# Early convolution blocks copied out of PSUM, keys rounded and half of the masked tiles made on VectorE, and four groups of matmuls set later

## The chip, the cores and the metric

The kernel runs on one core of a Trainium2 chip. The metric is the device time of one execution in microseconds (us), as the median of a few runs. The engines are named as in the profile: PE is TensorE's matmul, PEld its weight load, DVE is VectorE, ACT is ScalarE, POOL is GpSimd and SP is SyncE, which here issues most of the DMAs.

## The reference

One layer of a hybrid backbone on 1024 latent tokens and 256 context tokens of width 1024, in float32. The normed and modulated tokens go through one input projection, whose columns belong to two groups. Group A is a gated DeltaNet of 4 heads of 128 in two scan directions, group B is a two-dimensional neighbourhood attention of 8 heads of 64.

```python
h = modulate(rms_norm(x, w), shift, scale)        # 1280 x 1024
p = h @ w_in                                      # q, k, v, z, a, b of group A; q, k, v of group B
# group A
q, k, v = split(silu(conv5(p_qkv)))               # depthwise, 5 taps, centred, context and latent apart
k = k / sqrt(sum(k * k) + EPS)
g = -exp(A_log) * softplus(a + dt_bias);  beta = sigmoid(b)
decay = exp(gam_i - gam_j) where i >= j, else 0   # gam: running sum of g within a chunk
m = where(strict, (k * beta) @ k.T * decay, 0)
u, w = solve(eye + m, [v * beta, k * beta * exp(gam)])   # one triangular system a chunk
# then a scan over the chunks, forward and backward
# group B
q, k = rms_norm(q) * 64 ** -0.5, rms_norm(k)      # heads of 64, then the windowed softmax
```

Behind that come an output projection, a gated residual and a SwiGLU. The change concerns the stage up to about 400 us: the input projection, the preparation of the triangular systems, and what runs beside them.

## The kernel before

**The in-projection.** Tokens lie along the free axis, features on the partitions. The modulated input is held as two float32r parts, `hh` (rounded) and `hl` (the rest), and so is each weight tile, `whi` and `wlo`; a product is three matmuls, hi by hi, hi by lo and lo by hi (`mm_part`, L413). `Block` makes 128 output columns for all tokens, in PSUM tiles `blk` of 256, 512 and 512 tokens (q and nq: only the two of 512). `Wide` makes 256 columns with the tokens on the partitions. The jobs run in this order: k0 and k1 together, k2, k3, z's second half, then nk0 to nk2, nv's first half, nk3, q0 to q3, nq0 to nq3 and the rest. The letters q, k, v, z are of group A, nq, nk, nv of group B.

**A block's life.** `prefetch` loads the raw weight into `wraw` (one buffer only), ScalarE casts it to `whi` (L203), POOL subtracts to get `wlo` (L204); for a `Wide` job two loads into the same `wraw` are cast to `zw` (L601) and subtracted (L602). The next load into `wraw` waits for the cast and the subtraction of the one before. `evac` takes the sums out of PSUM into `cacc`; for q, k and v it also does the convolution, centre tap first, then four more taps. While `len(psum) == 1`, that is for k0 to k3, ScalarE scales out of PSUM into `cacc` (L446) and VectorE reads the four outer taps from PSUM, per segment (L455); for later blocks ScalarE copies into `cr` (L461) and VectorE does all five taps from there (L465, L469). `silu`, `norm` and `finish` follow one or two jobs later. For nk, `norm` sums squares on PE (L502), takes a logarithm (L503) and an exponential (L507) on ScalarE, scales on VectorE (L510), and splits into float16 parts: cast on ScalarE (L515), subtraction on VectorE (L516). For k, `finish` transposes (L537) and multiplies keys with keys (L561, copied by ScalarE at L562), and POOL with VectorE sum the diagonal.

**Banks.** Up to z's end one pool of 8 PSUM banks serves everything. From nk0 on, `blk` has 4 banks, `m` 2 and `pr` 2.

**The background work.** Generators step along between the groups of matmuls: each `bg.step` of the job loop runs a generator to its next `yield`, and a `yield` with nothing else lets one group of the job's matmuls pass (an empty step). `decay_tables` forms the decays and multiplies them on PE (L842). `block_inverses` makes masked tiles `rc` of the two parts GH and GL of the decays (`rhs`, L865, 12 of them, on POOL), a product of each pair (L878) and an exponential on ScalarE (L880) into WK and W, then masks on VectorE (L885 to L892), transposes into N (L900, copied at L902), an elimination of 30 pairs of VectorE instructions on N (L910, L912), and transposes out of N (L922, copied to WK at L926). `preps` prepares the chunks: `fx` and `y` tiles, decay products (L1003) and exponentials (L1008), a product kk by e on VectorE (L1011), products with fx (L1024) and a short series of `y` products (L1035). A second generator, `modulation`, forms the second half of the adaLN vector: VectorE accumulates eight `wad` tiles into `acc2` (L236, L238), and PE sums it over the partitions against ones (L223).

Every engine works through its instructions in the order in which a scheduler puts them; PE, VectorE and ScalarE wait on semaphores for one another, and nothing overtakes on an engine.

## Time and profile before

| what | us |
|---|---|
| runs, median (of 3) | 1512.97 |
| runs, lowest and highest | 1512.54, 1517.85 |
| the profiled execution: span | 1510.6 |
| PE busy in the span | 1462.2 (97%) |
| VectorE, ScalarE, POOL busy | 996.8, 703.5, 236.7 |

The profiled execution's own time outside the profiler isn't recorded, so its span stands for it; the median of the runs lies 2.4 us above the span. A row of the timeline has the start, the duration, the engine, line and operation, the output and inputs, and in brackets the idle time before it with what ended that. A row of the waits has what PE was about to run, whose end it waited for, and the total, the number and the longest wait.

### The profile page before, as it was taken

The numbers are of one execution on the slowest core, as the hardware profiler recorded it, in microseconds if no ns is written. First come the engines' busy times: TensorE is split into PE (matmuls) and PEld (weight loads), VectorE is DVE, ScalarE is ACT, GpSimd is POOL, SyncE is SP. The second block draws the span as 40 slices with busy tenths as digits, with TensorE's granted clock in tenths as the row PEclk, the third lists the DMA queues.
The fourth block names the chain that finished last, engine by engine and source line by source line (L and its number), as shares of the span: only waits on it lengthen the run. The fifth ranks groups of instructions, "written<-read, shape, count | busy, mean of one in ns | idle before, by whom it ended". The sixth has DMA issues, their size and how long they took to land.

```text
span 1510.6 us, 23890 instructions
## 1 busy us (share of the span) xinstructions
PE 1462.2 (97%) x8702; PEld 1223.5 (81%) x8702; DVE 996.8 (66%) x1716; ACT 703.5 (47%) x1389; POOL 236.7 (16%) x286
## 2 busy tenths in 40 slices
PE   6999999999999998999999999999999999999998
PEld 3788797877788877887878888888888888888887
DVE  5773589875463745778867389766665567598652
ACT  5453442456663246656853284333333334354440
POOL 1054601456652201111210000000000000000000
PEclk9999999999999999999999999999999999999999
DMA  9274122778665569998539205433333335798742
GB/s 389 75 215 143 54 78 72 244 222 248 195 191 174 157 187 291 290 263 279 163 112 343 79 28 166 141 105 105 105 105 105 105 105 174 260 360 279 251 140 84
DMA packets 205398, 267.36 MB, mean 177 GB/s; under 512 B 15968, under 2 KB 113760, under 8 KB 204256
## 3 DMA queue, kind: packets, MB, share of 16 engines
q1 hardware_dynamic: 197680, 260.01, 53.2%
q10 hardware_dynamic: 7600, 5.81, 1.2%
q8 instruction: 69, 1.13, 0.3%
q14 instruction: 49, 0.40, 0.1%
HBM read 201.02 MB, written 68.94 MB: 179 GB/s over the span
## 4 chain that ended last, share of the span: by engine, by line
PE 51%; ACT 1%; DVE 1%; issue 0%; DMA 0%; POOL 0%; DVEq 0%; POOLq 0%; ACTq 0%
PE ps L1398 28%; PE ps L1741 14%; PE ps L1527 3%; PE ps L1375 1%; PE ps L1549 1%; PE sc L332 1%; PE sc L322 1%; PE sc L309 1%; PE ps L1252 0%; PE ps L1261 0%; DMA z<-z_d 0%; ACT sq L1302 0%; ACT bt L315 0%; DVE bt L313 0%; PE ps L223 0%
## 5 line engine op out<-in xcount | busy, mean ns | idle before, releaser
L1459 ACT CAST uhi<-wq 128x512 fp32r<-128x512 f32 x101 | 61.3, 622 | 135.9 <-issue 84.6
L413 PE MATMUL blk<-hh,whi 128*128 128x512 f32 (+1 forms) x410 | 121.0, 389 | 1.6 <-ACT kk L562 1.4
L1459 ACT CAST uhi<-ws 128x512 fp32r<-128x512 f32 x91 | 54.0, 621 | 146.3 <-PE ps L1398 91.4
L413 PE MATMUL blk<-hl,whi 128*128 128x512 f32 (+1 forms) x410 | 113.4, 370 | 0.3 <-DVE hl L729 0.3
L609 PE MATMUL blk<-zw,hh 128*128 128x256 f32 (+1 forms) x576 | 112.3, 289 | 1.0 <-ACT cr L461 1.0
L413 PE MATMUL blk<-hh,wlo 128*128 128x512 f32 (+1 forms) x410 | 112.0, 370 | 0.6 <-POOL wlo L204 0.6
L1460 DVE TENSOR_TENSOR ulo<-wq,uhi 128x512 fp32r<-128x512 f32 x101 | 67.6, 688 | 59.1 <-ACT uhi L1459 32.7
L1398 PE MATMUL ps<-hT,uhi 128*128 128x512 f32 x336 | 103.7, 390 | 0.0
L1398 PE MATMUL ps<-lT,uhi 128*128 128x512 f32 x336 | 103.4, 389 | 0.0
L1398 PE MATMUL ps<-hT,ulo 128*128 128x512 f32 x336 | 103.4, 389 | 0.0
L609 PEld LDWEIGHTS blk<-zw,hh 128*128 128x128 f32 x576 | 90.7, 189 | 4.1 <-ACT cr L461 1.4
L1398 PE MATMUL ps<-hB,uhi 128*128 128x512 f32 x288 | 89.1, 390 | 0.0
L1398 PE MATMUL ps<-lB,uhi 128*128 128x512 f32 x288 | 88.7, 389 | 0.0
L1398 PE MATMUL ps<-hB,ulo 128*128 128x512 f32 x288 | 88.7, 389 | 0.0
L413 PEld LDWEIGHTS blk<-hh,wlo 128*128 128x128 f32 x410 | 71.0, 188 | 14.8 <-POOL wlo L204 0.9
L413 PEld LDWEIGHTS blk<-hl,whi 128*128 128x128 f32 x410 | 71.2, 188 | 14.4 <-DVE hl L729 0.8
L609 PE MATMUL blk<-zw,hl 128*128 128x256 f32 (+1 forms) x288 | 81.9, 284 | 0.0
L413 PEld LDWEIGHTS blk<-hh,whi 128*128 128x128 f32 x410 | 67.6, 190 | 16.8 <-issue 3.8
L204 POOL TENSOR_TENSOR wlo<-wraw,whi 128x1024 fp32r<-128x1024 f32 x18 | 44.8, 2488 | 186.8 <-ACT whi L203 186.5
L1398 PEld LDWEIGHTS ps<-lT,uhi 128*128 128x128 f32 x336 | 63.1, 188 | 13.1
L1398 PEld LDWEIGHTS ps<-hT,ulo 128*128 128x128 f32 x336 | 63.1, 188 | 13.1
L1398 PEld LDWEIGHTS ps<-hT,uhi 128*128 128x128 f32 x336 | 62.9, 188 | 13.0
(361 smaller groups left out, 3500.7 us busy)
## 6 DMA issues: line engine op xcount, KB each, us to landing
wq<-w_fo SPq DMA_DIRECT2D x99, 256.0 KB, 4.2
wq<-w_gu SPq DMA_DIRECT2D x88, 256.0 KB, 2.9
wad<-wa SPq DMA_DIRECT2D x64, 256.0 KB, 4.3
bt<-rpb SPq DMA_DIRECT2D x64, 192.0 KB, 3.9
t_d<-g SPq DMA_DIRECT2D x22, 512.0 KB, 3.5
fr<-t_d SPq DMA_DIRECT2D x44, 256.0 KB, 4.9
f_d<-g SPq DMA_DIRECT2D x33, 256.0 KB, 2.1
fr<-f_d SPq DMA_DIRECT2D x33, 256.0 KB, 4.2
```

Of the source, the lines that this page charges most:

```text
L204: lo_engine.tensor_tensor(o, r, h.bitcast(F32), OP.subtract)
L309: s = pe.matmul(sc[:, u * 640 + n0:u * 640 + n1], q, ks[i], start=i == 0, stop=i == 1)
L322: pe.transpose(sc[:, u * 640 + j * 128:u * 640 + (j + 1) * 128], bt[:, j * 128:(j + 1) * 128], ident)
L332: pe.matmul(sc[u * ND:u * ND + ND, 1280:1408], vv, pt[:, j * 128:(j + 1) * 128], start=j == 0, stop=j == 4)
L413: pe.matmul(o, ww[:, k], xx[k][:, s], start=k == 0 and j == 0, stop=k == KT - 1 and j == 2)
L609: pe.matmul(p[:, :c1 - c0], x[k][:, s], ww[:, k, c0:c1], start=k == 0 and j == 0, stop=k == KT - 1 and j == 2)
L1375: pe.matmul(o, w[wi][:, k], parts[xi][k][:, s], start=k == 4 and j == 0, stop=k == 3 and j == 2)
L1398: pe.matmul(o, w[wi][:, k], x[xi][:, k], start=first and k == 0 and j == 0, stop=k == n - 1 and j == 2, skip_group_check=True)
L1459: act.copy(hi, self.raw[key])
L1460: dve.tensor_tensor(lo, self.raw[key], hi.bitcast(F32), OP.subtract)
L1527: pe.matmul(o, w[wi][:, k], parts[xi][k][:, s], start=k == 0 and j == 0, stop=k == KT - 1 and j == 2)
L1741: pe.matmul(o[b], w[wi][:, b], F[xn, p][xi], start=n in (0, 1, 5) and p == 0 and j == 0, stop=p == NFB // 2 - 1 and j == 2, skip_group_che ...
```

## The change

It makes eight edits, all in this stage:

1. k0 to k3: ScalarE copies the three segments into `cr`, then makes the centre tap from `cr` (256 and 1024 wide), and VectorE reads the four outer taps of the context and of the latent part from `cr`. The nk and nq evacuation uses a copy in place of an activation with scale 1.
2. nk: the float16 cast of the keys is VectorE's instead of ScalarE's.
3. k3: the three copies of keys by keys are VectorE's instead of ScalarE's.
4. The masked tiles of GL are VectorE's; those of GH stay on POOL.
5. Five empty steps instead of four ahead of the decay products.
6. Eight empty steps instead of seven ahead of the transposes out of N.
7. Seven empty steps instead of four ahead of the sums of `acc2` with ones.
8. For the first chunk's preparation: four steps instead of two ahead of the fx products, and LATE 5 instead of 7 ahead of the decay products.

```diff
@@ modulation
             if sums == 1:
-                for _ in range(4):
+                for _ in range(7):
                     yield
                 reduce(q, prev)
@@ Block.evac
-                if not conv or len(psum) == 1:
+                if not conv:
                     for p, s0, n in self.pss:
-                        act.activation(acc[:, s0:s0 + n], p[:, :n], AF.Copy, scale=cw[:, blk, 2:3] if conv else 1.0)
-                if not conv:
+                        act.copy(acc[:, s0:s0 + n], p[:, :n])
                     return
-                if len(psum) == 1:
-                    for p, s0, n in self.pss:
-                        lo, hi = (0, CT) if s0 < CT else (CT, T)
-                        for tap in (0, 1, 3, 4):
-                            o = tap - 2
-                            d0, d1 = max(lo, s0 - o), min(hi, s0 + n - o)
-                            dve.scalar_tensor_tensor(acc[:, d0:d1], p[:, d0 + o - s0:d1 + o - s0],
-                                                     cw[:, blk, tap:tap + 1], acc[:, d0:d1],
-                                                     op0=OP.mult, op1=OP.add)
-                    return
+                early = len(psum) == 1
                 raw = cp.tile([128, T], F32, name="cr", tag="cr", bufs=2)
                 for p, s0, n in self.pss:
                     self.last = act.copy(raw[:, s0:s0 + n], p[:, :n])
                 for lo, hi in ((0, CT), (CT, T)):
                     if hi <= t0:
                         continue
-                    dve.tensor_scalar(acc[:, lo:hi], raw[:, lo:hi], cw[:, blk, 2:3], None, op0=OP.mult)
+                    if early:
+                        act.activation(acc[:, lo:hi], raw[:, lo:hi], AF.Copy, scale=cw[:, blk, 2:3])
+                    else:
+                        dve.tensor_scalar(acc[:, lo:hi], raw[:, lo:hi], cw[:, blk, 2:3], None, op0=OP.mult)
@@ Block.norm
                 if isk:
-                    act.copy(h16, u)
+                    dve.tensor_copy(h16, u)
@@ Block.finish
-                        gates.append(act.copy(kk[:, g:g + m].rearrange("p c d -> p (c d)"), p[:, :m * 128]))
+                        kkf = kk[:, g:g + m].rearrange("p c d -> p (c d)")
+                        if (kind, i) == ("k", 3):
+                            dve.tensor_copy(kkf, p[:, :m * 128])
+                        else:
+                            gates.append(act.copy(kkf, p[:, :m * 128]))
@@ decay_tables
-            for _ in range(4):
+            for _ in range(5):
                 yield
@@ block_inverses, rhs
-                            pool.tensor_tensor(
+                            (pool if gg is GH else dve).tensor_tensor(
                                 rc[:, :n],
@@ block_inverses
-                for _ in range(7):
+                for _ in range(8):
                     yield
                 U = WK.rearrange("p d u i -> p (d u) i")
@@ preps, prep
-                    yield 1
-                    yield 1
+                    for _ in range(4 if i == 0 else 2):
+                        yield 1
@@ preps
-                LATE, stores, tick = 7, [], [0]
+                LATE, stores, tick = 5, [], [0]
```

Since `gates` lists one group of copies less, the exponentials of `decay_tables`, which wait for the last of them, now follow another instruction.

The edits move instructions on ScalarE too. The first place is around the end of block nk1. Here is ScalarE's order in the kernel before, from the second half's mask exponentials (`W1` from `m`) over the second cast to `zw`, nk1's copies to `cacc`, and the logarithms of nk0 (`cr`), to the cast of the next `whi`:

```order
L880 ACTIVATE W1_1447<-m_1552 128x512 [waits PE_49]
L880 ACTIVATE W1_1447<-m_1569 128x512 [waits PE_49]
L601 CAST zw_1632<-wraw_1637 128x8x128 [waits DMAHW2_49]
L880 ACTIVATE W1_1447<-m_1582 128x256 [waits PE_49]
L446 ACTIVATE cacc_1608<-blk_1498 128x256 [waits PE_49]
L446 ACTIVATE cacc_1608<-blk_1499 128x512 [waits PE_49]
L446 ACTIVATE cacc_1608<-blk_1500 128x512 [waits PE_49]
L503 ACTIVATE cr_1490<-m_1612,bias_62 128x256 [waits PE_49]
L479 ACTIVATE cr_1630<-cacc_1608 128x1280 [waits Activation_49]
L503 ACTIVATE cr_1490<-m_1615,bias_62 128x512 [waits PE_49]
L503 ACTIVATE cr_1490<-pr_1618,bias_62 128x512 [waits PE_49]
L203 CAST whi_1796<-wraw_1795 128x1024 [waits DMAHW3_49]
```

The same place on ScalarE in the changed kernel, whose line numbers are three lower here (the first cast to `zw`, the first row, stands one row ahead of the piece above in the kernel before):

```order
L598 CAST zw_1627<-wraw_1628 128x8x128 [waits DMAHW1_49]
L598 CAST zw_1627<-wraw_1632 128x8x128 [waits DMAHW2_49]
L877 ACTIVATE W1_1452<-m_1557 128x512 [waits PE_49]
L877 ACTIVATE W1_1452<-m_1574 128x512 [waits PE_49]
L877 ACTIVATE W1_1452<-m_1587 128x256 [waits PE_49]
L203 CAST whi_1785<-wraw_1784 128x1024 [waits DMAHW3_49,PE_49,Pool_49]
L446 COPY cacc_1603<-blk_1486 128x256 [waits PE_49]
L446 COPY cacc_1603<-blk_1487 128x512 [waits PE_49]
L446 COPY cacc_1603<-blk_1488 128x512 [waits PE_49]
L496 ACTIVATE cr_1478<-m_1607,bias_62 128x256 [waits PE_49]
```

The second cast to `zw` has moved ahead of all three exponentials, and the cast to `whi` ahead of nk1's copies and the logarithms.

The second place is on ScalarE around the transposes out of N, which are copied to WK, and block q0's SiLU (`cacc` on `cacc`, behind the table load). In the kernel before:

```order
L926 COPY WK_603<-m_2371 128x80x4 [waits PE_49]
L926 COPY WK_603<-m_2377 128x80x4 [waits PE_49]
L926 COPY WK_603<-m_2392 128x80x4 [waits PE_49]
L926 COPY WK_603<-m_2398 128x80x4 [waits PE_49]
L515 CAST hl16_2347<-cacc_2236 128x1280 [waits DMAHW6_49,DMAHW0_49,DVE_49]
L926 COPY WK_603<-m_2410 128x80x4 [waits PE_49]
L926 COPY WK_603<-m_2416 128x80x4 [waits PE_49]
L476 ACT_TABLE_LOAD
L476 ACTIVATE cacc_2327<-cacc_2327 128x1024 [waits DVE_49]
L926 COPY WK_603<-m_2428 128x80x4 [waits PE_49]
```

In the changed kernel:

```order
L923 COPY WK_603<-m_2382 128x80x4 [waits PE_49]
L923 COPY WK_603<-m_2388 128x80x4 [waits PE_49]
L923 COPY WK_603<-m_2400 128x80x4 [waits PE_49]
L923 COPY WK_603<-m_2406 128x80x4 [waits PE_49]
L469 ACT_TABLE_LOAD
L469 ACTIVATE cacc_2323<-cacc_2323 128x1024 [waits DVE_49]
L923 COPY WK_603<-m_2418 128x80x4 [waits PE_49]
L472 ACTIVATE cr_2351<-cacc_2323 128x1024 [waits Activation_49]
L923 COPY WK_603<-m_2424 128x80x4 [waits PE_49]
L923 COPY WK_603<-m_2436 128x80x4 [waits PE_49]
```

The cast has left ScalarE, and the table load and the SiLU have moved up by two copies, ahead of the fifth.

The third place is on VectorE, at the end of the elimination and in q0's taps (`cacc` from `cr`), with nk3's scaling (L510, then L503) and subtraction or cast. In the kernel before:

```order
L912 TENSOR_TENSOR N_1443<-N_1443,tt_1768 80x4x30 [waits DVE_49]
L465 TENSOR_SCALAR cacc_2327<-cr_2328,cw_73 128x1024 [waits Activation_49]
L469 SCALAR_TENSOR_TENSOR cacc_2327<-cr_2328,cw_73,cacc_2327 128x1022 [waits DVE_49]
L469 SCALAR_TENSOR_TENSOR cacc_2327<-cr_2328,cw_73,cacc_2327 128x1023 [waits DVE_49]
L510 SCALAR_TENSOR_TENSOR cacc_2236<-cacc_2236,qkw_74,cr_2240 128x1280 [waits Activation_49]
L469 SCALAR_TENSOR_TENSOR cacc_2327<-cr_2328,cw_73,cacc_2327 128x1023 [waits DVE_49]
L469 SCALAR_TENSOR_TENSOR cacc_2327<-cr_2328,cw_73,cacc_2327 128x1022 [waits DVE_49]
```

In the changed kernel:

```order
L909 TENSOR_TENSOR N_1448<-N_1448,tt_1822 80x4x30 [waits DVE_49]
L458 TENSOR_SCALAR cacc_2323<-cr_2324,cw_73 128x1024 [waits Activation_49]
L462 SCALAR_TENSOR_TENSOR cacc_2323<-cr_2324,cw_73,cacc_2323 128x1022 [waits DVE_49]
L462 SCALAR_TENSOR_TENSOR cacc_2323<-cr_2324,cw_73,cacc_2323 128x1023 [waits DVE_49]
L503 SCALAR_TENSOR_TENSOR cacc_2230<-cacc_2230,qkw_74,cr_2234 128x1280 [waits Activation_49]
L462 SCALAR_TENSOR_TENSOR cacc_2323<-cr_2324,cw_73,cacc_2323 128x1023 [waits DVE_49]
L508 CAST hl16_2343<-cacc_2230 128x1280 [waits DMAHW6_49,DMAHW5_49,DMAHW7_49,DMAHW0_49,DVE_49]
L462 SCALAR_TENSOR_TENSOR cacc_2323<-cr_2324,cw_73,cacc_2323 128x1022 [waits DVE_49]
```

A cast now stands ahead of the last of q0's taps.

## The prediction

> **What bounds the kernel now.** I read the page first, for the engine that fills the span, then TensorE's (PE's) waits by releaser, because only they can give time back, and then the timeline of each engine around the waits that the change touches.
>
> ```profile
> span 1510.6 us, 23890 instructions
> PE 1462.2 (97%) x8702; PEld 1223.5 (81%) x8702; DVE 996.8 (66%) x1716; ACT 703.5 (47%) x1389; POOL 236.7 (16%) x286
> ```
>
> PE is busy for 97% of the span, and the change leaves its 8702 matmuls as they are: neither the reference's work nor a tile's shape changes. So the time can move only by what PE waits, and by the clock it gets. These are its waits in the part of the program that the change touches, in us, with the count and the longest.
>
> ```profile
> PE m L223 <- DVE acc L238: 2.0, 1, 2.0
> PE m L537 <- DVE cacc L455: 1.7, 1, 1.7
> PE m L900 <- ACT N L902: 1.4, 1, 1.4
> PE blk L413 <- ACT kk L562: 1.4, 1, 1.4
> PE m L922 <- DVE N L915: 1.3, 1, 1.3
> PE pr L1024 <- DVE kk L1011: 1.2, 2, 0.8
> PE m L878 <- POOL rc L865: 1.1, 3, 0.7
> PE blk L413 <- POOL wlo L204: 0.6, 1, 0.6
> PE m L842 <- DVE G L821: 0.4, 1, 0.4
> PE m L922 <- DVE N L912: 0.3, 1, 0.3
> ```
>
> Their sum is 11.4 us. The L223 wait costs more than its 2.0 us, as the next rows show: the wait itself, a second one of almost the same length, and the stretches behind each (columns: busy time and count of PE, PEld, DVE, ACT, POOL, then the granted clock, the DMA share and GB/s).
>
> ```profile
> 292.99 0.35 PE L223 MATMUL m<-ones,acc 128*128 128x1 f32 x2 [2.01 <-DVE acc L238]
> 428.04 0.36 PE L1035 MATMUL pr<-y,kk 128*32 128x64 f32 x6 [1.92 <-DVE y L1037]
> 293.88:297.29 3.41, 3.41 (x10) 2.73 (x10) 3.13 (x4) 3.03 (x6) 3.37 (x4) 0.52 1.02 311
> 430.00:433.00 3.00, 3.00 (x23) 2.69 (x22) 0.77 (x1) 2.92 (x5) 3.00 (x4) 1.00 0.01 1
> ```
>
> Behind the 2.01 us wait PE ran 3.41 us at a clock of 0.52, which loses 3.41 x 0.48 = 1.6 us; behind the 1.92 us wait it kept 1.00. So about 2 us of waiting is where a wait may or may not cost another 1.6 us here. [...]
>
> **The change part by part: what goes.** Early blocks leave PSUM in three ScalarE copies, so the five taps no longer hold banks: the 1.7 us at L537 goes, as PE waited there for a bank that VectorE's taps still read. The weight halves' wait (0.6) goes with VectorE's and POOL's shifted work, the decay step (0.4) with one more empty step, the masked tiles' 1.1 with two engines making them. The kk copies of block k3 leave ScalarE's queue for VectorE's; no row shows a VectorE copy of that shape, so of its 1.4 I take half, 0.7, bounds 0 and 1.4. The transposes into N (1.4), those out of N (1.3 + 0.3, one step more), the L223 sums (2.0 + 1.6, three steps more) and the fx products (1.2, two steps more) all move later. In all 4.5 us ahead of block nk2 and 7.8 us behind its start.
>
> **What comes: ScalarE's order.** ScalarE works in order, and the order changes around block nk1: both casts of `zw` now stand ahead of the three exponentials of the second half's masks, and the cast of the next `whi` ahead of the three `cacc` copies that free nk1's banks. Each of these casts waits for a load into the one buffer `wraw`, and that load waits for the cast and POOL's subtraction before. In before's trace the chain runs like this (ScalarE, then POOL, then SyncE's queue).
>
> ```profile
> 156.81 1.05 ACT L203 CAST whi<-wraw 128x1024 fp32r<-128x1024 f32 x1 [0.56 <-PE blk L413]
> 165.37 1.05 ACT L601 CAST zw<-wraw 128x1024 fp32r<-128x1024 f32 x1 [4.34 <-DMA wraw<-w_nv]
> 174.54 1.05 ACT L601 CAST zw<-wraw 128x1024 fp32r<-128x1024 f32 x1 [5.50 <-DMA wraw<-w_nv]
> 175.50 0.38 ACT L880 ACTIVATE W<-m 128x256 f32<-128x256 f32 x1
> 175.77 1.35 ACT L446 ACTIVATE cacc<-blk 128x256 f32<-128x256 f32 x3
> 182.28 1.05 ACT L203 CAST whi<-wraw 128x1024 fp32r<-128x1024 f32 x1 [2.48 <-DMA wraw<-w_nqk]
> ...
> 165.56 2.29 POOL L865 TENSOR_TENSOR rc<-GL,cst 128x512 fp32r<-128x512 f32 x1
> 167.81 2.39 POOL L602 TENSOR_TENSOR zw<-wraw,zw 128x1024 fp32r<-128x1024 f32 x1
> 175.67 2.36 POOL L602 TENSOR_TENSOR zw<-wraw,zw 128x1024 fp32r<-128x1024 f32 x1 [4.32 <-ACT zw L601]
> ...
> 178.06 0.54 SPq L199 DMA_DIRECT2D wraw<-w_nqk  x1
> ```
>
> A link with nothing in its way is the last one: 182.28 - 174.54 = 7.7 us (cast 1.05, subtraction 2.36, load 4.2). The one before took 9.2, because a masked tile stood ahead of POOL's subtraction; with half of these tiles on VectorE I take three clean links, 23.2 us. The chain starts when PE leaves nk0, and PE is there 0.6 + 1.7 + 0.7 + 0.4 = 3.4 us earlier: 156.8 - 3.4 = 153.4. The third cast then runs from 176.6 to 177.7, and the first and smallest of the three `cacc` copies (1.35 together) is done about 0.4 later, at 178.1. Until then PE lacks a bank for the second segment of nk2. PE itself would be ready sooner:
>
> ```profile
> 170.83 0.38 PE L878 MATMUL m<-rc,mr 128*128 128x256 f32 x1 [0.68 <-POOL rc L865]
> 177.35 1.15 PE L413 MATMUL blk<-hh,whi 128*128 128x256 f32 x3
> ```
>
> Nk2 begins at 177.35 before; less 3.4 and the masked tiles' 1.1 that would be 172.9. So about 5.2 us of new waits stand here, in two pieces: first the last mask product, whose bank waits for an exponential behind the second cast (153.4 + 15.5 + 1.05 = 170.0, and 0.5 for an exponential twice as wide as that of 0.38, by estimate: 170.5; PE comes between 166.5 and 168.6, since an extra step puts matmuls ahead: some 2 us), then nk2's second segment, the other 3 us or so. PE is 178.1 - 177.35 = 0.8 us **behind** before at this point: the 4.5 us gained are gone. Ends: were each load as short as the page's quickest weight load,
>
> ```profile
> wq<-w_gu SPq DMA_DIRECT2D x88, 256.0 KB, 2.9
> ```
>
> three loads would save 3.9 us, so 3.1 ahead; were the chain as long as before (25.5 us), 2.3 more, so 3.1 behind. Clock: the 2 us piece may halve it (0.5, a third of 1.6), the 3 us piece probably does (1.4).
>
> **What comes: VectorE.** The four casts of the rounded keys move from ScalarE to VectorE; the nearest row is the same cast on ScalarE. Around it, the last rows of the elimination, block q0's taps and its SiLU stand like this.
>
> ```profile
> 265.40 1.26 ACT L515 CAST hl<-cacc 128x1280 f16<-128x1280 f32 x1 [1.10 <-DVE cacc L510]
> 266.57 0.74 ACT L926 COPY WK<-m 128x320 f32<-128x320 f32 x2
> 267.33 1.28 ACT L476 ACT_TABLE_LOAD   x1
> 268.63 1.06 ACT L476 ACTIVATE cacc<-cacc 128x1024 f32<-128x1024 f32 x1
> ...
> 267.80 1.48 DVE L516 TENSOR_TENSOR hl<-cacc,hl 128x1280 f16<-128x1280 f32 x1
> ...
> 267.39 1.01 PE L922 MATMUL m<-cst,N 80*128 80x80 f32 x8
> ...
> 190.00:260.00 70.00, 68.71 (x430) 59.86 (x429) 62.02 (x63) 26.49 (x43) 7.24 (x3) 1.00 0.22 62
> ```
>
> VectorE is busy 62.02 of the 70 us that hold the elimination, a chain of its own instructions; two casts in it add 2.5 us (0 to 2.5), and it starts about 2.7 later (0.8 and the clock's 1.9). Of the transposes' wait of 1.6, which an extra step and other moved matmuls cover by an estimated 2.7, some 0.8 stays (0 to 2.5). Then ScalarE again: the table load and SiLU of q0 now follow the fourth copy into WK instead of the sixth. SiLU needs q0's taps, which ended about 267.8; in the new order they end 2.7 + 2.5 + 1.3 later, at 274.3, SiLU at 275.4 and the copy behind it at 275.8. PE would come for its bank at 267.39 + 2.7 + 2.7 + 0.8 = 273.6. I take 2.5 us (0 to 6), and 1.1 of clock. Two more: copies into N behind the next `whi` cast, 0.8 (0 to 1.4, the L900 row); the second sum at L223, whose accumulations come later on VectorE, 0.8 (0 to 2.5).
>
> **What comes: the taps.** They read SBUF in place of PSUM.
>
> ```profile
> L455 DVE SCALAR_TENSOR_TENSOR cacc<-blk,cw,cacc 128x512 f32<-128x512 f32 x16 | 11.8, 739 | 0.0
> L469 DVE SCALAR_TENSOR_TENSOR cacc<-cr,cw,cacc 128x1023 f32<-128x1023 f32 x6 | 8.0, 1334 | 0.0
> L910 DVE TENSOR_TENSOR tt<-N 80x336 f32<-80x336 f32 x2 | 5.3, 2642 | 0.1
> L912 DVE TENSOR_TENSOR N<-N,tt 80x336 f32<-80x336 f32 x2 | 1.0, 504 | 0.1
> ```
>
> Eight taps of 739 ns become four of 1334: 5.9 us become 5.3 per block, nearly nothing. The two 80x336 rows are as long as each other in elements and differ by 2.1 us, with POOL's subtraction beside the long one. [...] By the two rows block k0's SiLU, and PE's first transposes behind it, could come up to 2.1 us late; as the mean of 1334 has such collisions in it already, I take 0.3.
>
> **The sum.** Up to nk2 +0.8. Behind it -7.8 for the waits that go; the taps' 0.3 counts with what comes; +0.5 + 1.4 + 1.1 clock, +0.8 N copies, +0.8 elimination, +2.5 SiLU, +0.8 second sum, +0.3 taps, together +8.2. Net +1.2 us: a span of 1511.8. The median of the runs before, 1512.97, lies 2.4 above the profiled span, so 1514.2.
>
> **The rivals.** *The removed waits really go.* If the loads are short (3.1 ahead at nk2 in place of 0.8 behind) and the new waits behind it come to a quarter, 2 us, the net is -3.1 - 7.8 + 2 = -8.9: 1504.1; all 12.3 us without any new wait would be 1500.7. For it: each wait in the list has an answer in the diff, and what I put in its place hangs on a queue order and on loads that start at other times than in the trace. Against it: the last load there took 4.2 us from issue to cast, and the two `zw` casts waited 4.34 and 5.50 for theirs.
>
> *VectorE becomes the bound from 190 to 275* (slower). The casts and the later start add up on the elimination, PE waits 2.5 at the transposes and 6 at SiLU, with the clock halved behind both (3.3), so 11.8 where the sum has 4.4: +1.2 + 7.4 = 8.6, 1521.6. It decides once VectorE ends the elimination over 8 us later than before. For it: 62.02 of 70 busy. Against it: the extra steps give PE other work.
>
> *The clock holds.* If waits of 2 to 3 us leave the clock alone, as the one of 1.92 did, the 3.0 us of clock in the sum vanish: -1.8, so 1511.2, still within no change; the 2.01 us row speaks against it. [...] *The change does less than it says*: the banks stay held at L537 and the 1.7 stays, 1515.9, also no change.
>
> **How the numbers follow.** About 0.5% (7.6 us) is what a measurement of this kernel tells from no change, so 1505.4 to 1520.5 is "same". The forecast has 0.35; with the clock holding (0.08) and the change doing less (0.03) the band has 0.46. The removed waits go: 0.34, and nearly all of it below 1505.4. VectorE or ScalarE's queue as a bound: 0.20, above 1520.5. The range takes the first rival's centre with half of its way to 1500.7 and the second rival's centre: 1502 to 1522. The likeliest case's own range is 1506 to 1519.
>
> **What would show it.** Right: in the profile after, the L537, L878 and L842 waits gone; PE waiting for an exponential W and then for `cacc` or `whi` near 170 to 178, about 5 us together, with a clock near 0.5 behind it; a wait for SiLU's copy WK near 273. Wrong: PE at the start of nk2 before 175, or no PE wait over 2 us between 165 and 280 (then the first rival), or a transposes' wait over 2 us at L919 (the second).

## The result, and the profile after

The changed kernel takes 1532.98 us (median of 4 runs, 1529.75 to 1535.53) where the kernel before takes 1513.12 beside it (1512.54 to 1517.85): a ratio of 1.0114, with an interval from 1.0095 to 1.0134. By that ratio it is slower by about 17 us, by the medians by 20: above the end of the range at 1522 either way. The forecast was no change, and the likeliest other sign was a gain. Each profile is of one execution (here the quickest of the four), so kernels are compared by the ratio, and the traces say where the time goes.

The top of the page after, for the same two rows as of before:

```profile
span 1528.0 us, 23873 instructions
PE 1467.5 (96%) x8702; PEld 1228.8 (80%) x8702; DVE 1010.8 (66%) x1713; ACT 700.7 (46%) x1389; POOL 239.8 (16%) x280
```

The span grew by 17.4 us, and PE's busy time by 5.3 of these with the same 8702 matmuls: I put that part down to the clock, granted at 0.92, 0.97 and 0.94 in three of the stages below where before has 1.00, 1.00 and 0.98. The other 12.1 us are new waiting. PE's waits by releaser after (total, count, longest):

```profile
PE m L554 <- ACT vt L532: 6.3, 1, 6.3
...
PE m L875 <- ACT W L877: 3.1, 1, 3.1
...
PE m L919 <- ACT WK L923: 2.2, 1, 2.2
...
PE m L653 <- ACT abT L627: 2.0, 1, 2.0
PE pr L1021 <- DVE y L1034: 2.0, 2, 1.5
PE pr L997 <- POOL rg L985: 2.0, 2, 1.2
PE blk L413 <- ACT cacc L446: 1.5, 1, 1.5
...
PE blk L624 <- ACT vt L532: 1.0, 1, 1.0
...
PE blk L413 <- DVE nA L797: 0.8, 1, 0.8
PE m L919 <- DVE N L912: 0.6, 1, 0.6
...
PE m L919 <- DVE N L909: 0.3, 1, 0.3
```

The waits that the change was forecast to remove are gone, all but a rest of 0.9 us of the 1.6 at the transposes out of N. The longest wait of this stage stands where no term of the sum had one: in front of the last of k0's keys by keys (L554 now). These matmuls need a bank that ScalarE has to empty first, by copying k0's transposed keys (L532).

Where the time went shows in the windows by stage. First after, then the same stretches of time of before (190 to 260 of before is in the prediction); columns as there: PE's busy time is the second figure, the granted clock the seventh. The changed kernel is late by some 11 us from 130 on, so its later stretches hold work that is somewhat earlier in the program.

```profile
64.00:130.00 66.00, 56.59 (x346) 50.15 (x345) 46.76 (x41) 29.96 (x48) 38.75 (x24) 0.92 0.49 146
130.00:190.00 60.00, 54.58 (x327) 47.78 (x325) 35.10 (x63) 18.74 (x47) 27.76 (x28) 0.97 0.35 104
190.00:260.00 70.00, 70.00 (x452) 62.07 (x452) 54.02 (x54) 25.16 (x43) 6.68 (x3) 1.00 0.24 66
260.00:345.00 85.00, 77.55 (x436) 63.70 (x435) 70.80 (x72) 39.04 (x67) 37.22 (x38) 0.94 0.61 186
345.00:430.00 85.00, 84.03 (x558) 66.64 (x557) 44.97 (x63) 51.36 (x98) 45.88 (x54) 1.00 0.75 228
```

```profile
64.00:130.00 66.00, 63.41 (x425) 56.95 (x424) 44.20 (x60) 29.71 (x54) 32.88 (x31) 1.00 0.60 181
130.00:190.00 60.00, 55.45 (x313) 46.19 (x312) 30.58 (x55) 24.21 (x46) 30.67 (x28) 1.00 0.26 77
...
260.00:345.00 85.00, 81.43 (x513) 68.11 (x514) 68.27 (x67) 43.99 (x75) 41.39 (x42) 0.98 0.75 232
345.00:430.00 85.00, 82.85 (x572) 66.33 (x571) 48.12 (x67) 55.78 (x108) 51.01 (x59) 1.00 0.73 219
```

Busy time times clock says, roughly, what PE got done in a stage. From 64 to 130 it falls from 63.4 to 52.1 (56.59 x 0.92): 11.3 us lost. From 130 to 190 it falls by 2.5, from 260 to 345 by 6.9 (79.8 to 72.9). The other two win 1.3 and 1.2. Together that is 18.2 us lost, close to the span's 17.4. So there are two losses to explain: a big one at 64 to 130, where the sum had a gain of 2.3 us (the waits for `wlo` and at L537) and 0.3 us for the taps, and one at 260 to 345, where its terms add up to a gain of 1.2. The 2.5 from 130 to 190 belong to nk1's casts, which were forecast.

The timeline tells of the first one. After: POOL's subtraction for k3's weights, VectorE beside it, SyncE's load for z, ScalarE, PE.

```profile
74.07 10.45 POOL L204 TENSOR_TENSOR wlo<-wraw,whi 128x1024 fp32r<-128x1024 f32 x1 [6.36 <-ACT whi L203]
...
68.58 11.20 DVE L462 SCALAR_TENSOR_TENSOR cacc<-cr,cw,cacc 128x255 f32<-128x255 f32 x14
79.70 0.74 DVE L238 SCALAR_TENSOR_TENSOR acc<-wad,sc,acc 128x512 f32<-128x512 f32 x1
80.36 1.27 DVE L462 SCALAR_TENSOR_TENSOR cacc<-cr,cw,cacc 128x1022 f32<-128x1022 f32 x1
81.56 0.74 DVE L238 SCALAR_TENSOR_TENSOR acc<-wad,sc,acc 128x512 f32<-128x512 f32 x1
82.33 2.73 DVE L238 SCALAR_TENSOR_TENSOR acc<-wad,sc,acc 128x512 f32<-128x512 f32 x1
...
84.55 0.33 SPq L597 DMA_DIRECT2D wraw<-w_z  x1
...
88.42 1.10 ACT L598 CAST zw<-wraw 128x1088 fp32r<-128x1088 f32 x1 [11.84 <-DMA wraw<-w_z]
89.42 1.34 ACT L532 COPY vt<-m 128x512 f32<-128x512 f32 x3
...
90.05 1.23 PE L554 MATMUL m<-cacc 128*128 128x128 f32 x4 [6.29 <-ACT vt L532]
```

The same steps before:

```profile
74.15 2.40 POOL L204 TENSOR_TENSOR wlo<-wraw,whi 128x1024 fp32r<-128x1024 f32 x1 [5.13 <-ACT whi L203]
...
76.58 0.33 SPq L600 DMA_DIRECT2D wraw<-w_z  x1
...
79.84 1.10 ACT L601 CAST zw<-wraw 128x1088 fp32r<-128x1088 f32 x1 [1.46 <-DMA wraw<-w_z]
80.85 1.34 ACT L539 COPY vt<-m 128x512 f32<-128x512 f32 x3
```

The same subtraction takes 10.45 us instead of 2.40 and ends at 84.52 instead of 76.55. All that time VectorE runs taps and `acc2` steps, each with two inputs in SBUF. Each starts 0.07 to 0.08 us before the one ahead of it ends (79.70 + 0.74 = 80.44, the next at 80.36), until the step at 81.56 ends at 82.30 and the next starts at 82.33. From there that next step takes 2.73 where the two ahead of it took 0.74 each, and POOL is done 2.2 us after its start. So, read from these rows, POOL stood still for about 8 us (10.45 - 2.40) and got in at the first break: not one instruction of VectorE's held it off, but a whole row of them, of which the single ones shown take 0.74 and 1.27 us. `wraw` has one buffer, so the load for z starts at 84.55 instead of 76.58; ScalarE works in order, and after 11.84 us without work runs z's cast at 88.42 and the copies of the keys behind it, at 89.42; PE waits for the bank that these empty.

Before's trace shows the other case. The instructions of the elimination have two SBUF inputs too, but where one of them follows another, it starts 0.03 to 0.04 us after the one ahead of it has ended. POOL's subtraction comes in at such a break, of 0.04 us, each of the three times that it meets them (197.78, 244.53 and 255.81). At the second one VectorE runs from 243.79 to 244.77, and the next instruction, 0.98 us long at 212.79, starts at 244.81 and has to wait:

```profile
244.53 2.50 POOL L204 TENSOR_TENSOR wlo<-wraw,whi 128x1024 fp32r<-128x1024 f32 x1 [44.39 <-ACT whi L203]
...
244.81 3.07 DVE L912 TENSOR_TENSOR N<-N,tt 80x792 f32<-80x792 f32 x1
```

The other two times it is the 80x336 instruction of the prediction's rows that comes second. So these rows show VectorE waiting for POOL, and not what POOL does behind instructions without a break between them.

### The profile page after: what moved, and what is told of

Same layout as the page of the kernel before. It is cut to its first block, busy times and chain, and to the rows that moved or that the text cites. A ratio compares the mean times of both kernels' runs of the same rounds, so it can differ in the third digit from the quotient of the medians.

```text
span 1528.0 us, 23873 instructions
## 1 busy us (share of the span) xinstructions
PE 1467.5 (96%) x8702; PEld 1228.8 (80%) x8702; DVE 1010.8 (66%) x1713; ACT 700.7 (46%) x1389; POOL 239.8 (16%) x280
## 4 chain that ended last, share of the span: by engine, by line
PE 51%; ACT 1%; DVE 0%; issue 0%; DVEq 0%; ACTq 0%
PE ps L1395 28%; PE ps L1738 14%; PE ps L1524 3%; PE ps L1372 1%; PE ps L1546 1%; PE sc L332 1%; PE sc L309 1%; PE sc L322 1%; PE ps L1270 0%; PE ps L1249 0%; PE ps L1258 0%; ACT sq L1299 0%; DVE bt L313 0%; PE ps L223 0%; ACT pt L325 0%; PE ps L1275 0%
## 5 line engine op out<-in xcount | busy, mean ns | idle before, releaser
L462 DVE SCALAR_TENSOR_TENSOR cacc<-cr,cw,cacc 128x1023 f32<-128x1023 f32 (+3 forms) x80 | 91.3, 1172 | 19.0 <-ACT cacc L456 18.1
L204 POOL TENSOR_TENSOR wlo<-wraw,whi 128x1024 fp32r<-128x1024 f32 x18 | 53.5, 2974 | 197.5 <-ACT whi L203 194.2
```

The costliest lines, as they stand in the source:

```text
L204: lo_engine.tensor_tensor(o, r, h.bitcast(F32), OP.subtract)
L462: dve.scalar_tensor_tensor(acc[:, d0:d1], raw[:, d0 + o:d1 + o], cw[:, blk, tap:tap + 1], acc[:, d0:d1], op0=OP.mult, op1=OP.add)
```

## Experiments: which part costs what

The theory going in was that two edits cost independently of each other: the evacuation (by VectorE's row of instructions with two SBUF inputs, beside which POOL's subtraction takes 10.45 us, and z's load) and the empty steps (by waits that come back). The rival was that it is the cast and the masked tiles on VectorE, that is VectorE as the bound.

**The changed kernel with the old evacuation** (edits 2 to 8):

```diff
+                        act.activation(acc[:, s0:s0 + n], p[:, :n], AF.Copy, scale=cw[:, blk, 2:3] if conv else 1.0)
...
+                if len(psum) == 1:
...
-                        act.copy(acc[:, s0:s0 + n], p[:, :n])
...
+                        for tap in (0, 1, 3, 4):
...
-                early = len(psum) == 1
...
```

> The changed kernel with the early blocks' evacuation put back (taps read PSUM). Theory A: the taps that read two SBUF inputs hold POOL off, its subtraction for k3 takes 10.45 us instead of 2.4, the load of z's weight starts 8 us late, and the cast that waits for it stands ahead of the key copies on ScalarE; so here the subtraction is back near 2.4 us, PE's 6.3 us wait at 90 us is gone with the half clock behind it and the waits of 1.0 and 2.0 us that follow, and the time is 1519 to 1523 us. Rival B: the loss comes from the new order of ScalarE and VectorE behind 150 us; then this kernel stays within 3 us of 1533.

Measured: 1523.88, ratio 1.0053 [1.0036, 1.0069]. POOL's row:

```profile
75.60 2.41 POOL L204 TENSOR_TENSOR wlo<-wraw,whi 128x1024 fp32r<-128x1024 f32 x1 [5.08 <-ACT whi L203]
```

With taps that read PSUM the subtraction is back at 2.41 us, and the waits for L532, of 6.3 and 1.0, and the one for `abT` are gone. 0.53% of the 1.14% stay, so the evacuation is not all of it.

**The new evacuation alone**, the reverse:

```diff
                 for p, s0, n in self.pss:
                     self.last = act.copy(raw[:, s0:s0 + n], p[:, :n])
...
+                    if early:
+                        act.activation(acc[:, lo:hi], raw[:, lo:hi], AF.Copy, scale=cw[:, blk, 2:3])
+                    else:
                         dve.tensor_scalar(acc[:, lo:hi], raw[:, lo:hi], cw[:, blk, 2:3], None, op0=OP.mult)
```

> The kernel before with the new early evacuation alone. Theory A: POOL's subtraction for k3 takes about 10 us and the time is 6 to 12 us above before, 1519 to 1525 us. Rival B: the 1.7 us wait for a bank at the key transposes goes and nothing comes in its place, 1510 to 1513 us.

Measured: 1522.81, ratio 1.0062 [1.0041, 1.0083], that is 9.4 us (0.0062 x 1513). The chain is there in full, POOL and PE:

```profile
74.64 10.74 POOL L204 TENSOR_TENSOR wlo<-wraw,whi 128x1024 fp32r<-128x1024 f32 x1 [6.08 <-ACT whi L203]
...
90.87 1.22 PE L554 MATMUL m<-cacc 128*128 128x128 f32 x4 [6.25 <-ACT vt L532]
```

**The empty steps alone** (edits 5 to 8), to see whether the rest of the loss is theirs:

```diff
-                for _ in range(4):
+                for _ in range(7):
...
-            for _ in range(4):
+            for _ in range(5):
...
-                for _ in range(7):
+                for _ in range(8):
...
+                    for _ in range(4 if i == 0 else 2):
...
-                LATE, stores, tick = 7, [], [0]
+                LATE, stores, tick = 5, [], [0]
```

> The kernel before with the empty steps and LATE alone (edits 5 to 8). Waits of 0.4, 1.6, 2.0 (with its clock 1.6) and 1.2 us go, 6.8 us in all, if nothing replaces them: 1506 us. The trace of the kernel with the old evacuation says that something does: one exponential behind the second zw cast, q0's SiLU ahead of the WK copies (2.2 us and clock) and the decay tiles of the first chunk (2.0 us, LATE): then 1511 to 1516 us.

Measured: 1523.30, ratio 1.0049 [1.0031, 1.0066], 7.4 us. Its waits:

```profile
PE m L922 <- ACT WK L926: 4.1, 1, 4.1
...
PE m L502 <- ACT W L880: 2.6, 1, 2.6
PE pr L1000 <- POOL rg L988: 2.3, 3, 1.2
PE pr L1024 <- DVE y L1037: 1.9, 2, 1.4
```

The sums of `acc2`, the copies into N, the transposes out of N and the decay step no longer wait (2.0, 1.4, 1.6, 0.4 before). In their place PE waits 4.1 for a copy to WK, 2.6 for an exponential W, 2.3 for POOL's `rg` tiles, and 2.7 more for `y` (1.4 at the products with fx, L1024, and 1.3 at the `y` products, L1035). More comes back than went.

**The three moves between engines** (edits 2, 3 and 4), then two of them alone:

```diff
-                    act.copy(h16, u)
+                    dve.tensor_copy(h16, u)
...
+                        if (kind, i) == ("k", 3):
+                            dve.tensor_copy(kkf, p[:, :m * 128])
...
-                            pool.tensor_tensor(
+                            (pool if gg is GH else dve).tensor_tensor(
```

> The kernel before with the three moves between engines alone: cast, k3's key copies and masked tiles on VectorE (edits 2, 3 and 4), no steps and the old evacuation. If the whole loss is the evacuation's and the steps' (9.4 and 7.5 us): within 2 us of before. If the moves need the steps, or load VectorE together: 1516 us or more.

Measured: 1513.47, ratio 0.9992 [0.9983, 1.0002]. These edits are free. Evacuation and steps together make 0.62% + 0.49% = 1.11%, where the whole change has 1.14%: the two losses add up within their intervals of 0.2% each way, with no third.

The masked tiles alone:

```diff
-                            pool.tensor_tensor(
+                            (pool if gg is GH else dve).tensor_tensor(
```

> The kernel before with the masked tiles of GL on VectorE, alone. By the prediction the waits of 1.1 us for masked tiles go: 1511 to 1513 us. Under rival B VectorE's and ScalarE's order behind 150 us gets worse with it: 1516 us or more.

Measured: 1513.98, ratio 0.9994 [0.9982, 1.0006]. The mask products' wait on POOL falls from 1.1 to 0.9, and the next group waits 1.4 for the exponential W instead of 0.2: the gain is given back within 6 us, since W hangs on ScalarE's queue and that is no earlier.

The cast alone:

```diff
-                    act.copy(h16, u)
+                    dve.tensor_copy(h16, u)
```

> The kernel before with the keys' float16 cast on VectorE, alone. If the cast is what loads VectorE in the elimination (second rival of the prediction): transposes out of N wait 2 us or more longer, 1515 to 1518 us. If the cast is harmless: within 2 us of before, as VectorE does it in 0.82 us and saves ScalarE 1.26 us each.

Measured: 1515.68, ratio 1.0001 [0.9986, 1.0016].

```profile
267.08 0.82 DVE L515 CAST hl<-cacc 128x1280 f16<-128x1280 f32 x1
```

The cast takes 0.82 us on VectorE, not ScalarE's 1.26. The wait for N's copies (1.4) goes, and the transposes behind the elimination wait 2.6 instead of 1.3. The rival with VectorE as the bound falls: its mechanism is there, with 1.3 us and not 7.4, and in the changed kernel the transposes wait 0.9 and for the WK copy 2.2, where the rival had 2.5 and 6.

## Experiments: does VectorE's row hold POOL off?

**The new evacuation with the last tap read from PSUM.** If VectorE holds POOL off by instructions with two SBUF inputs, one instruction with a single SBUF input in every four should let POOL in; if POOL is slowed by anything else in the evacuation, its row stays long. Everything else stays as in the evacuation alone.

```diff
+                        if early and tap == 4:
+                            for p, s0, n in self.pss:
+                                e0, e1 = max(d0, s0 - o), min(d1, s0 + n - o)
+                                if lo <= s0 < hi and e0 < e1:
+                                    dve.scalar_tensor_tensor(acc[:, e0:e1], p[:, e0 + o - s0:e1 + o - s0],
...
+                            continue
```

> The kernel before with the new early evacuation, but the last of the four taps reads PSUM again, so that instructions with one SBUF input stand between those with two. If VectorE's instructions with two SBUF inputs shut POOL out until one comes that has not (a lock): POOL's subtraction for k3, begun near 74 us, ends behind k0's last tap, near 78 us, and takes 3 to 5 us in place of 10.7; PE's 6.3 us wait falls under 1.5 and the time is 1511 to 1516 us. If the two engines only share bandwidth: the subtraction shrinks by the share of the PSUM taps, to 8 us or so, PE still waits 4 us, 1519 us or more.

Measured: 1517.64, above the range expected for the lock, ratio 1.0019 [1.0000, 1.0038]. POOL's subtraction and VectorE beside it:

```profile
75.31 2.54 POOL L204 TENSOR_TENSOR wlo<-wraw,whi 128x1024 fp32r<-128x1024 f32 x1 [5.83 <-ACT whi L203]
...
70.34 0.47 DVE L470 SCALAR_TENSOR_TENSOR cacc<-cr,cw,cacc 128x255 f32<-128x255 f32 x1
...
75.50 1.39 DVE L466 SCALAR_TENSOR_TENSOR cacc<-blk,cw,cacc 128x510 f32<-128x510 f32 x2
76.82 1.31 DVE L470 SCALAR_TENSOR_TENSOR cacc<-cr,cw,cacc 128x255 f32<-128x255 f32 x1
```

POOL starts 0.2 us before the two PSUM taps (`blk`, at 75.50) and takes 2.54. The tap from `cr` behind them waits in its turn: one of 0.47 us (70.34) takes 1.31 here, to 78.13, where POOL's subtraction runs until 77.85. Of the 9.4 us 6.5 are gone; the 2.9 left have an interval from 0 to 5.8. PE still waits 1.8 us for the copies of the keys in this trace (1.3 and 0.5), which may be a part of them.

**The same in the changed kernel**:

```diff
+                        if early and tap == 4:
+                            for p, s0, n in self.pss:
...
+                            continue
```

> The changed kernel with the last of the early taps read from PSUM again, nothing else. If POOL is shut out only by an unbroken row of two-input instructions on VectorE: its subtraction takes 2.5 to 5 us in place of 10.45, PE's 6.3 us wait with its half clock goes, and the time falls by the 6 to 8 us that the same step gave in the kernel before with the new evacuation: 1525 to 1527 us. If the changed kernel's loss is not the subtraction's: above 1530 us.

Measured: 1524.35, ratio 1.0077 [1.0055, 1.0098]; the changed kernel had 1.0114, so 5.6 us come back (each interval is 3 us either way). POOL, then PE at the keys by keys:

```profile
73.23 2.40 POOL L204 TENSOR_TENSOR wlo<-wraw,whi 128x1024 fp32r<-128x1024 f32 x1 [6.01 <-ACT whi L203]
...
81.20 1.16 PE L562 MATMUL m<-cacc 128*128 128x128 f32 x8 [0.56 <-ACT vt L540]
```

Of the waits for these copies, 6.3 and 1.0 us, 0.56 is left here and 1.2 at later transposes (106.8). In the stage from 64 to 130 PE is busy 62.3 us at a clock of 1.00, where the changed kernel had 56.6 at 0.92. That is 10 us more work done; from 260 to 345 it is 2.4 us less than in the changed kernel (76.66 x 0.92 = 70.5), so a part of what is won here is lost again further on.

**VectorE makes k3's subtraction itself**, so that POOL has none to make beside the row:

```diff
-                jobs[n + 1].prefetch()
+                jobs[n + 1].prefetch(**({"lo_engine": dve} if n + 1 == 3 else {}))
```

> The changed kernel with k3's subtraction (wlo) on VectorE instead of POOL; all else as in the changed kernel. Theory A: the subtraction is short again, the load of z's weight starts 5 us or more earlier, PE's wait at 90 us falls from 6.3 to under 1.5, and the time is 1521 to 1527 us, though the taps are still the new ones. Rival B, and a third one, that the taps themselves are too slow on VectorE: within 3 us of 1533.

Measured: 1528.59, ratio 1.0075 [1.0051, 1.0098]; its median lies above what was expected, and is of 5 runs. The instruction that waited 8 us takes 1.22 on VectorE (at 78.84), and PE waits at two other places:

```profile
102.50 0.29 PE L624 MATMUL blk<-hh,zw 128*16 128x256 f32 x1 [1.79 <-ACT zw L598]
...
105.06 0.41 PE L624 MATMUL blk<-hh,zw 128*16 128x256 f32 x2 [2.15 <-POOL zw L599]
```

The load for z starts at 80.08, but its cast comes at 85.91 and its subtraction at 94.51, so that z's second load starts at 97.09. The edit also moved other work: the cast of `zw` now stands behind copies of keys on ScalarE, and the subtraction behind the tiles of the diagonal on POOL. So it takes the big wait away, but doesn't tell the part of POOL's subtraction from that of the order.

## Experiments: why the steps give nothing

The theory: the stage behind nk2 is bound by chains through ScalarE, VectorE and POOL, so that groups of PE set later only meet the next link. The rival: one of the steps is bad and the others gain.

**Without LATE, and without the ones at the decay and at N** (edits 3, 7 and the first half of 8):

```diff
-                for _ in range(4):
+                for _ in range(7):
                     yield
                 reduce(q, prev)
...
+                        if (kind, i) == ("k", 3):
+                            dve.tensor_copy(kkf, p[:, :m * 128])
...
+                    for _ in range(4 if i == 0 else 2):
+                        yield 1
```

> The kernel before with three edits that remove a wait without moving ScalarE's queue at nk1 or at the WK copies: k3's key copies on VectorE, seven steps ahead of the acc2 sums, four steps ahead of the first fx products (LATE stays 7). Waits of up to 1.4, 3.6 and 1.2 us go: 1506 to 1509 us. If every removed wait is given back further on: within 2 us of before.

Measured: 1515.46, ratio 0.9998 [0.9981, 1.0014]. PE's first decay products of `preps`, and POOL's tiles for them:

```profile
291.40 0.49 PE L1004 MATMUL pr<-rg,mr 128*128 128x512 f32 x1 [2.38 <-POOL rg L992]
292.84 0.50 PE L1004 MATMUL pr<-rg,mr 128*128 128x512 f32 x1 [0.95 <-POOL rg L992]
...
290.31 1.04 POOL L992 TENSOR_TENSOR rg<-GH,cst 128x512 fp32r<-128x512 f32 x1 [11.51 <-DVE acc L238]
```

The `acc2` wait (2.0 and 1.6 of clock) is gone, and 3.6 us for `rg` (the two waits shown and one of 0.27) stand in the same ten us, where the clock is at 0.85 and 0.81: all of it is given back at once. POOL could not start `rg` before 290.31, though it had been idle for 11.5 us.

**The same three edits with LATE 10**, to let the tiles be ready:

```diff
-                LATE, stores, tick = 7, [], [0]
+                LATE, stores, tick = 10, [], [0]
```

> The three edits of the earlier run (k3's key copies on VectorE, seven steps ahead of the acc2 sums, four ahead of the first fx products) with LATE 10, so that PE reaches the first decay products some 5 us later in its own order. If the 3.6 us wait for POOL's tiles there took back the three edits' gain, it shrinks below 1 us and the time is 4 to 6 us under that of before, near 1508. If the gain is lost elsewhere: within 2 us of before.

Measured: 1515.75, ratio 1.0007 [0.9991, 1.0024]. The `rg` waits fall to 1.9, not below 1, without a clock loss there (1.00 from 285 to 310), and no time comes out of it. Where it is lost this run doesn't show.

**One edit alone, or one left out.** First edit 6 alone:

```diff
-                for _ in range(7):
+                for _ in range(8):
```

> The kernel before with eight empty steps ahead of the transposes out of N, alone (edit 6). ScalarE's table load and q0's SiLU then stand behind the fourth WK copy. If that is what costs time in the steps: the transposes' first wait of 1.6 us is gone, a wait of 2 to 4 us for a WK copy comes at the seventh group, mostly with 1.7 us of half clock, and the time is 1515 to 1519 us. If one step more is just harmless: 1511 to 1513 us.

Measured: 1517.10, ratio 1.0010 [1.0000, 1.0020]. Of the wait for N (1.6) 0.35 stays, and one for WK (1.8) has come in. At the `y` products, 309 us in, PE waits 4.4 for POOL's `y` where it waited 1.2 for VectorE's kk products before.

LATE 5 alone:

```diff
-                LATE, stores, tick = 7, [], [0]
+                LATE, stores, tick = 5, [], [0]
```

> The kernel before with LATE 5 in place of 7, alone. The first chunk's decay products come two steps, some 3.5 us, sooner on PE, but POOL can make their tiles only once the elimination's memory is free, so PE waits 2 to 3.5 us for them, with 1.7 us of half clock: 1515 to 1519 us. If LATE is harmless: 1511 to 1515 us.

Measured: 1519.44, ratio 1.0018 [1.0000, 1.0035]; the waits of 2 to 3.5 us for POOL's tiles that were expected aren't in its trace, and no new wait behind nk2 is over 0.8 us. Whether LATE 5 costs anything alone, from 0 to 5.3 us by the interval, stays open.

The steps without edit 6, shown against the steps alone:

```diff
-                for _ in range(8):
+                for _ in range(7):
```

> The kernel before with edits 5, 7 and 8 (all steps but the eighth ahead of the transposes out of N). The eight steps alone cost about 1.5 us and all steps together 7.5. If the WK wait of 4.06 us with its half clock, which all steps showed, needs the eighth step: that wait falls under 2 us and the time is 1515 to 1518 us. If the steps cost in total whatever one is left out, because each moves SiLU or POOL's tiles against PE: 1519 us or more.

Measured: 1525.51, ratio 1.0072 [1.0052, 1.0092], not better than with it (their intervals overlap). The wait for WK is down to 1.8 from 4.1, and 3.9 us for `rg` have come in, with the clock halved behind:

```profile
300.00:305.00 5.00, 3.94 (x11) 2.83 (x11) 4.96 (x4) 2.70 (x6) 4.92 (x5) 0.50 0.98 299
305.00:310.00 5.00, 5.00 (x18) 4.52 (x19) 4.65 (x5) 0.39 (x2) 4.88 (x4) 0.50 0.64 204
```

The steps without edit 7, again against the steps alone:

```diff
-                for _ in range(7):
+                for _ in range(4):
                     yield
                 reduce(q, prev)
```

> The kernel before with edits 5, 6 and 8 (all steps but the three ahead of the acc2 sums). If the three steps cause the waits for POOL's decay tiles (PE comes to them sooner once the acc2 wait is gone): these fall from 2.3 us to under 1, the acc2 wait of 2 us is back, and the time is 1518 to 1521 us. If LATE causes them: they stay near 2.3 us or move, and the time is 1521 us or more.

Measured: 1523.38, ratio 1.0060 [1.0036, 1.0083]. The `acc2` wait is back with 1.9, `rg` is down to 0.2, WK stands at 4.0: about the same sum in other places.

No subset of the steps that was run gained, and leaving out edit 6 or 7 made the losing set no better. So the half of the rival by which the others gain isn't borne out. The other half isn't settled: edit 5 and LATE 5 are both in every set of steps that lost 7 us or more, edit 5 was never run alone, and no losing set was run again with just one of the two left out. The wait for LATE's own tiles, `rg`, can't be the whole reason, for without edit 7 it is 0.2 us and the loss is 9.1.

Nor is the place of the loss the same in every kernel. From 260 to 345 PE gets 79.8 us of work done before (81.43 x 0.98), 71.6 with the steps alone (76.15 x 0.94), but 78.4 with all the steps, the moves between engines and the old evacuation (79.96 x 0.98). That the steps as a whole cost time is measured; that each removed wait returns at the next link of its chain is read from single traces. A shorter chain itself, by a second buffer for `wraw` for example, was not tried.

## Why the prediction was wrong, point by point

**The step that failed: the taps.** It took 0.3 us, bounds 0 to 2.1, as an estimate from two rows of the elimination, for taps that "read SBUF in place of PSUM". It looked at one side only: at VectorE's instructions that grow beside POOL's, which is what the 80x336 rows show (2642 and 504 ns). It never asked what POOL's instruction loses, and who waits for it. That costs 9.4 us by the evacuation alone, of which 6.5 go (5.6 in the changed kernel) when one tap in four reads PSUM. The bound failed for the same reason: it was the length of one instruction, where VectorE has a row of 11 us. The rows of before could have told the place: POOL's 2.40 us stood at 74.15, beside the taps and between two loads into one buffer.

**The second step that failed: -7.8 behind nk2.** The waits are gone as forecast, and what stands in their place was put at 6.0 us with the clock's 1.1. The steps alone, which remove the same waits and the 0.4 at the decay, come out as a loss of 7.4. The forecast had one of the new waits, WK's: 2.16 us measured against 2.5. It lacked POOL's `rg` tiles (2.0 in the changed kernel, 0.2 to 3.9 in the experiments) with the clock behind them (0.68 and 0.64 over ten us), and 2.7 more for `y` (1.5 and 1.2). These waits were measured; why the steps together lose more than they remove stays open in part, as said above.

**Nk1's casts: right.** About 5.2 us in two pieces, an exponential W and then the bank's `cacc`, with half a clock behind:

```profile
182.30:185.80 3.50, 3.47 (x11) 3.05 (x12) 2.22 (x2) 0.75 (x2) 1.83 (x1) 0.54 0.06 16
```

Measured are 3.1 for W at 182 us and 1.5 for `cacc` at 190, 4.7 together, some 12 us later than forecast since the loss ahead delays both. The three links of the chain take 24.2 us (from the cast at 164.18 to that at 188.40) against 23.2. Of the two waits the first halved the clock (3.5 x 0.46 = 1.6 us), the second didn't (1.00 from 189.8 to 193.3). The forecast had the sizes the other way round, 2 and 3, and 1.9 of clock. The experiment with the old evacuation has the same two waits (3.0 and 1.7), so they owe nothing to the loss ahead of them; the steps alone have a wait for W too (2.6, in front of nk0's sums of squares).

**The smaller terms.** Of the kk copies' 1.4 half stayed by forecast, 0.8 by the trace (`nA`). The elimination was to leave 0.8 and left 0.9. Copies into N (0.8) and the second sum (0.8) were to wait and didn't. The cast was to take 1.26 and takes 0.82.

**The rivals.** That the removed waits really go was given as much chance as the forecast. They do go, without a gain: the argument "each wait in the list has an answer in the diff" speaks of that list alone, and not of what comes behind. VectorE as the bound had the right sign by another mechanism, which the moves between engines measure as nothing. The clock doesn't hold: behind waits of 2.0 us and more it fell each time in this stage of the changed kernel (6.3: 0.67, 3.1: 0.54, 2.2: 0.71, 2.0: 0.75, each over the next 3.5 to 5 us).

## What to carry to other kernels

When an operand moves from PSUM to SBUF, list what POOL runs at that time and price its wait by the length of the whole row of two-input VectorE instructions, not by one of them (here POOL's 2.40 us became 10.45 beside 14 taps of 11.20 us and what followed them); then follow whoever waits for POOL, above all where one buffer and an engine working in order pass the delay on (here 8.0 us to z's load and 6.3 us to PE). A wait that goes only counts as gained when the next link of the same chain (copy, exponential, tile) is earlier as well: take the sum from where the chain ends, not from the list of waits. One tap in four that reads PSUM was enough here to let POOL in (2.40 and 2.54 us); so was, as read from traces, a break of 0.03 to 0.04 us between two instructions.

## What the runs showed of the hardware

- POOL's 2.4 us subtraction took 10.45 and 10.74 us beside a row of VectorE instructions with two SBUF inputs, and 2.40 to 2.54 where taps in the row read PSUM. That it gets in at a break between two such instructions is read from traces: one place in each of the two long cases (0.03 us in the changed kernel, 0.04 in the evacuation alone), and three in before's elimination (0.04 us). No run tested the break by itself.
- VectorE's instructions took longer beside POOL's subtraction too: an `acc2` step 2.73 us where the two ahead of it took 0.74, a tap from `cr` 1.31 instead of 0.47, an instruction of the elimination 3.07 instead of 0.98.
- In the changed kernel a wait of 1.5 us left the clock at 1.00, and behind one of 3.1 us it was 0.54 over 3.5 us, which loses 1.6 us; after the 2.0 us for `abT` and the 2.2 for WK it fell too (0.75 and 0.71 over the next five us). In before's trace a wait of 1.9 us left it at 1.00, and behind one of 2.0 it was 0.52. Behind two waits for `rg` of 0.7 and 1.2 us within 2 us it fell too, to 0.68 and 0.64 over ten us; what the clock counts there isn't settled.
